# Feed-forward of a two-layer trunk: two instead of three blocks of gate and up by the plain product

## The chip, the core and the metric

The kernel runs on one core of one Trainium2 chip. The metric is the device time of one launch in microseconds (us), taken as the median of several runs; lower is better.

## What is computed

The reference is a trunk of two layers over 1024 latent tokens and 256 context tokens of width 1024. Each layer is a token mixer (a gating group, a windowed attention, a recurrent scan) followed by a feed-forward part. Only the feed-forward part matters here:

```python
def swiglu(h, w_gu, w_down):
    gu = h @ w_gu
    return (jax.nn.silu(gu[..., :D_FF]) * gu[..., D_FF:]) @ w_down
```

`h` has 1280 rows in the first layer (256 of context, 1024 latent) and 1024 in the second, `D_FF` is 2816, and everything is float32.

## The kernel before, in words

**Precision.** A float32 product is made of three products: each operand is split into a high part (a rounded copy, made by ScalarE) and a low part (the rest, by a subtraction on VectorE). `mm3` issues high times high, high times low and low times high. So one product of a 128x128 weight tile with 512 columns is three matmuls.

**Gate and up, in 22 blocks.** A block `f` is 128 columns of gate and the 128 columns of up that belong to them. Two ways of making it stand side by side:

- The *plain* way, `gu_group` (L1506): for each group of tokens (a group of 256 context tokens in the first layer alone, two of 512 latent tokens), 2 times 8 tiles of 128x128 with three matmuls each. For the latent tokens that is 2 x 2 x 8 x 3 = 96 matmuls of 512 columns.
- The way by *seven products of halves*, `visit` (L1604): the four products of a 2x2 block product are made by seven products (`operands` lists them), each with 4 tiles of 128x128 over 512 columns and three matmuls a tile: 7 x 4 x 3 = 84 matmuls of 512 columns. The context tokens go the plain way in both, with 48 matmuls of 256 columns.

**What the seven products need first.** `t_sums` (L1523) makes sums of parts of `h` on VectorE and splits them (tiles `tt`, by way of a temporary `tx`), for each of four slices `kk` of the width and for each of the two latent groups: eight pieces. `t_last` (L1549) then writes the last sum over a part of `h` that the plain way has read until then. `prep` (L1561) does the same for the weights of a block: it loads gate (`wq`) and up (`wu`), makes two sums of them on GpSimd (tiles `wq`), and splits the operands into `wh` and `wl` (ScalarE L1583, VectorE L1584), two of them ahead of the visit and two in it. Products 1 and 2 of a visit use the split of gate itself, and product 1 is the first of the visit.

**Space.** Large tiles lie in 33 numbered slots. `alloc` takes the slot that has been free the longest and `rel` puts it at the end of the queue; this is settled when the program is written, and a tile that takes over a slot waits on the chip until the last reader of the old one is done. When the sums come to the slice `kk = 3`, `h` has 16 slots, the output tile one, the weights' up half of block 1 two (tiles `wsh`, `wsl`, since the small ring `wh` of six is full), the `tt` tiles of the slices 0 to 2 nine, and the tiles `t4` two. The three `tt` tiles of slice 3 take the last three free slots, and the two `tx` tiles of that slice, one for each group, take the slots of `wsh` and `wsl`. Three slots for `prep` (`own`) are allocated after the sums: these are the same two slots, first that of the first group's `tx` (for the load of gate), then that of the second group's (for the first sum of weights), and then the slot of a `t4` tile (for the second sum, used by products 3 and 7).

**The order around the change** (L1770 to L1803). The plain blocks 0 and 1 go over the groups first, beside the norm of the next group and the sums. Then `after_two` runs: blocks 0 and 1 over the last group, the release of `wsh` and `wsl`, and then the further plain blocks (`range(2, NCL)`, so block 2 alone). Its steps are interleaved with the sums' steps by `weave`. Behind that stand `t_last`, `own`, the preparation of the first visited block, and the visits:

```python
        more = [(wget(0), wget(0)) for _ in range(2, NCL)]
        own = []
        nxt = prep(NCL, side, own)
...
        def after_two():
            yield from gu2(gb)
            for f in range(2):
                rel(*[z for w in wf[f] for z in w[2]])
            for f in range(2, NCL):
                yield from plain(f)
        weave(after_two(), both(sums(gb, (0, 1)), sums(ga, (2,)), sums(gb, (2,)), sums(ga, (3,)), sums(gb, (3,))))
        for kk in range(4):
            t_last(kk)
        own += [alloc("wq") for _ in range(3)]
        run(nxt)
```

The instructions of each engine run in one fixed order, which a scheduler settles when the program is built; loads and stores are issued in order on SyncE's queue. Results of a block go to memory (`actd`) and are read again by the product with `w_down`, which does not know how a block was made.

Of the kernel before, what the change touches and what calls it, by code (L numbers as in the profile page):

```python
# [34 lines left out]
NLATE = 5  # L35
FA = 6, 7, 8, 9
NP = 2
NCL = 3
DOWN = [(0, 21), (1, 2, 3), (4, 5, 6), (7, 8, 9), (10, 11, 12), (13, 14, 15), (16, 17), (18, 19, 20)]
PPW = 111  # L40
C_DECAY = 0.3032653298563167
# [52 lines left out]
def trunk(ctx: ExitStack, tc: tile.TileContext, x, ctxt, cc, w_mod, pp, w_in, w_out, lng, lnb, sgw, sink,  # L94
# [21 lines left out]
    def rel(*ss):  # L116
        for s in ss:
            free.append(s.i)
# [118 lines left out]
    def wget(ahead=2, slots=False):  # L237
        if not ready:
            emit_w(slots)
        r = ready.popleft()  # L240
        while len(ready) < ahead and plan and plan[0]:
            emit_w(slots)
        return r
# [17 lines left out]
    def mod_blocks(l, q, k):  # L261
        c = 2048 * q
        return [(w_mod[l, k * 128:(k + 1) * 128, c + z * 1024:c + (z + 1) * 1024], 0, 1024) for z in range(2)]

    def plan_gu(l, f):
        w = w_gu[l].rearrange("(k p) c -> p k c", p=128)
        plan.append((w[:, :, f * 128:(f + 1) * 128], 8, 128))
        plan.append((w[:, :, DFF + f * 128:DFF + (f + 1) * 128], 8, 128))
# [5 lines left out]
    for l in range(L):  # L274
# [9 lines left out]
        if l == 0:  # L284
            for k in range(8):
                plan.extend(mod_blocks(0, 2, k))
        for f in range(NCL):
            plan_gu(l, f)
# [248 lines left out]
    def layer(l):  # L537
# [1023 lines left out]
        def prep(f, side, own):  # L1561

            w = W()
            side.append(w)
            new = lambda i: sp.tile([128, NTOK], F32, tag=f"s{own[i].i}", name=nm("wq"))[:, :1024]
            g = new(0)
            u = wp.tile([128, 1024], F32, tag="wr", name=nm("wu"), bufs=2)
            wv = w_gu[l].rearrange("(k p) c -> p k c", p=128)
            for z, t in enumerate((g, u)):
                D.dma_start(t.rearrange("p (a b) -> p a b", a=8), wv[:, :, z * DFF + f * 128:z * DFF + (f + 1) * 128])  # L1570
            yield
            a, b = new(1), new(2)
            G.tensor_tensor(a[:, 0:512], u[:, 0:512], u[:, 512:1024], op=ALU.add)  # L1573
            G.tensor_tensor(a[:, 512:1024], a[:, 0:512], g[:, 0:512], op=ALU.subtract)
            yield
            G.tensor_tensor(b[:, 0:512], g[:, 0:512], u[:, 0:512], op=ALU.subtract)
            G.tensor_tensor(b[:, 512:1024], g[:, 512:1024], a[:, 512:1024], op=ALU.subtract)
            yield
            raw, w.hi, w.lo = (g, u, a, b), [None] * 4, [None] * 4

            def split(i):
                w.hi[i], w.lo[i] = (wp.tile([128, 1024], F32R, tag="wh", name=nm(x), bufs=6) for x in ("wh", "wl"))
                S.activation(w.hi[i], raw[i], AF.Copy)  # L1583
                V.tensor_tensor(w.lo[i], raw[i], f32(w.hi[i]), op=ALU.subtract)  # L1584
            split(0)
            yield
            split(2)
            yield
            w.late = [lambda: split(3), lambda: split(1)]
# [183 lines left out]
        side = []  # L1773
# [4 lines that stand above are left out]
        def plain(f):  # L1778
            w = more.pop(0)
            for gi in gord:  # L1780
                yield from gu_group(f, gi, w, ft)
            rel(*[z for x in w for z in x[2]])
# [7 lines that stand above are left out]
# [6 lines left out]
        wd = {}  # L1796
        for f in range(NCL, NFF):
            w = side.pop()
# [173 lines left out]
```

## Time and profile before

| | |
|---|---|
| median of 3 runs | 3268.1 us |
| lowest, highest | 3267.36, 3279.27 us |
| the profiled execution | 3278.91 us |
| its span | 3277.1 us |
| mean granted clock of TensorE | 0.979 |

The span is from the first to the last instruction of the profiled execution. In rows of a timeline, the first number is the start in us from the beginning of the span and the second the duration in us; "x2" stands for two instructions merged into one row. In square brackets stands how long the engine sat idle before it, and what released it. The ends of matmuls are modelled, and neighbours overlap: what one matmul costs in a stream is read from the distance of starts.

### The profile page before, as it was taken

The page shows a single profiled execution, that of the slowest core. Times are in us where ns is not written, and L with a number is a line of the kernel's source. Part 1 is how long each engine was busy: PE and PEld are TensorE (multiplying, and loading weights), DVE is VectorE, ACT ScalarE, POOL GpSimd, SP SyncE. Part 2 cuts the span into 40 slices and gives each one's busy share as a digit, 9 for nine tenths or more (in the row PEclk, how much of TensorE's full clock was granted, in tenths as well). Part 3 has the DMA queues.
Part 4 walks back from the last instruction along what each step waited for, and adds up shares of the span by engine and source line. Part 5 has one row for each costly group of instructions (what it writes and reads, how often), then busy time and mean ns, then how long its engine had stood idle before and what let it go on. Part 6 is the DMA issues. An engine that isn't in the chain of part 4 may idle for free. (4 is left out here: it accounts for less than half of the span.)

```text
span 3277.1 us, 51928 instructions
## 1 busy us (share of the span) xinstructions
PE 3163.4 (97%) x19892; PEld 2571.4 (78%) x19892; DVE 2022.1 (62%) x3966; ACT 1386.3 (42%) x2874; POOL 528.0 (16%) x598
## 2 busy tenths in 40 slices
PE   7998999999999999999999998999999999999998
PEld 4777988777788888886687777878777788888887
DVE  3457869676474555554455657779676666666556
ACT  4455477665342222222112555477665432333211
POOL 2103101132012222210001202001122122231000
PEclk9997999999999999999999989999999999999999
DMA  5784322445511222235722366412445222223232
GB/s 215 228 257 142 97 62 66 116 136 193 209 57 64 68 71 70 70 131 186 259 85 80 107 217 188 138 58 84 110 128 197 86 76 83 89 79 135 94 106 96
DMA packets 395175, 403.95 MB, mean 123 GB/s; under 512 B 113456, under 2 KB 334640, under 8 KB 394928
## 3 DMA queue, kind: packets, MB, share of 16 engines
q1 hardware_dynamic: 394928, 400.64, 37.7%
q8 instruction: 157, 2.57, 0.3%
q14 instruction: 90, 0.74, 0.1%
HBM read 279.97 MB, written 120.59 MB: 122 GB/s over the span
## 5 line engine op out<-in xcount | busy, mean ns | idle before, releaser
L147 PE MATMUL mm<-h,wh 128*128 128x512 f32 (+1 forms) x1424 | 423.9, 381 | 3.3 <-ACT ntmp L399 2.3
L147 PE MATMUL mm<-wh,h 128*128 128x256 f32 x1472 | 331.4, 301 | 0.8 <-DVE rtmp L954 0.8
L147 PE MATMUL dd<-h,wh 128*128 128x256 f32 (+1 forms) x1312 | 321.4, 336 | 1.3 <-DVE h L408 0.7
L147 PEld LDWEIGHTS mm<-h,wh 128*128 128x128 f32 x1424 | 260.1, 192 | 60.9 <-issue 10.8
L147 PE MATMUL mm<-h,wl 128*128 128x512 f32 (+1 forms) x712 | 268.6, 377 | 1.1 <-DVE wl L232 1.1
L147 PEld LDWEIGHTS mm<-wh,h 128*128 128x128 f32 x1472 | 255.6, 199 | 16.1 <-issue 15.2
L147 PEld LDWEIGHTS dd<-h,wh 128*128 128x128 f32 x1312 | 227.6, 191 | 29.4 <-DVE h L408 1.1
L1583 ACT ACTIVATE wh<-wq 128x1024 fp32r<-128x1024 f32 x114 | 121.0, 1061 | 302.3 <-PE dd L147 113.8
L147 PE MATMUL dd<-h,wl 128*128 128x256 f32 (+1 forms) x656 | 219.4, 334 | 0.0
L147 PE MATMUL mm<-wl,h 128*128 128x256 f32 x736 | 215.3, 292 | 1.8 <-DVE wl L232 1.8
L1584 DVE TENSOR_TENSOR wl<-wq,wh 128x1024 fp32r<-128x1024 f32 x114 | 141.3, 1240 | 114.3 <-ACT wh L1583 114.3
L147 PE MATMUL dd<-tt,wh 128*128 128x512 f32 x608 | 188.1, 391 | 0.0
L179 POOL TENSOR_TENSOR ss<-ss,mh_sb 128x1 f32<-128x1 f32 x74 | 50.6, 684 | 845.9 <-DVE ss L376 843.6
L147 PEld LDWEIGHTS mm<-h,wl 128*128 128x128 f32 x712 | 136.2, 191 | 26.3 <-issue 1.5
L1705 DVE TENSOR_TENSOR yac<-yac,mm 128x512 f32<-128x512 f32 x126 | 86.3, 685 | 112.1 <-PE mm L147 111.8
L147 PEld LDWEIGHTS mm<-wl,h 128*128 128x128 f32 x736 | 146.8, 199 | 6.4 <-issue 4.1
L1705 DVE TENSOR_TENSOR yac<-yac,xx 128x512 f32<-128x512 f32 x126 | 86.2, 684 | 92.8 <-PE xx L147 92.6
L1573 POOL TENSOR_TENSOR wq<-wu 128x512 f32<-128x512 f32 x38 | 49.2, 1295 | 561.7 <-DVE wl L1584 477.7
L147 PEld LDWEIGHTS dd<-h,wl 128*128 128x128 f32 x656 | 124.9, 190 | 12.4
L147 PEld LDWEIGHTS dd<-tt,wh 128*128 128x128 f32 x608 | 111.7, 188 | 21.3
L147 PE MATMUL u<-bC,bC 128*128 128x128 f32 (+1 forms) x640 | 119.6, 305 | 0.0
L147 PE MATMUL dd<-tt,wl 128*128 128x512 f32 x304 | 118.3, 389 | 0.0
(372 smaller groups left out, 7794.1 us busy)
## 6 DMA issues: line engine op xcount, KB each, us to landing
wm<-in_w_mod SPq DMA_DIRECT2D x80, 512.0 KB, 5.0
wr<-in_w_down SPq DMA_DIRECT2D x44, 512.0 KB, 4.3
wr<-in_w_in SPq DMA_DIRECT2D x38, 512.0 KB, 4.6
cb<-ao SPq DMA_DIRECT2D x76, 256.0 KB, 2.4
wu<-in_w_gu SPq DMA_DIRECT2D x38, 512.0 KB, 3.7
wq<-in_w_gu SPq DMA_DIRECT2D x38, 512.0 KB, 3.7
ao<-rk SPq DMA_DIRECT2D x58, 256.0 KB, 3.9
xs<-xr SPq DMA_DIRECT2D x28, 512.0 KB, 2.7
```

Of the source, the lines that this page charges most:

```text
L147: T.matmul(o, lhsT=lhsT, rhs=rhs, start=start, stop=stop, skip_group_check=parts)
L179: G.tensor_tensor(dst, src, mh[:, :n], op=ALU.pow)
L1573: G.tensor_tensor(a[:, 0:512], u[:, 0:512], u[:, 512:1024], op=ALU.add)
L1583: S.activation(w.hi[i], raw[i], AF.Copy)
L1584: V.tensor_tensor(w.lo[i], raw[i], f32(w.hi[i]), op=ALU.subtract)
L1705: V.tensor_tensor(yac[t].t[:, c], yac[t].t[:, c], ps, op=ALU.add)
```

## The change

One constant is lowered, so that the plain way makes blocks 0 and 1 and the seven products make blocks 2 to 21, in both layers.

```diff
-NCL = 3
+NCL = 2
```

It is used in four places: the plan of loads (`plan_gu`), the list `more`, the loop of `after_two`, and the first block of `prep` and of the loop of visits. The tile slots are handed out in the same order as before, since the plain block 2 allocates none.

## Rows read from the trace of the kernel before

**Rows 1.** The page: TensorE's share of the span, and its granted clock.
```profile
PE 3163.4 (97%) x19892; PEld 2571.4 (78%) x19892; DVE 2022.1 (62%) x3966; ACT 1386.3 (42%) x2874; POOL 528.0 (16%) x598
...
PEclk9997999999999999999999989999999999999999
```

**Rows 2.** Stretches A:B of the visits: length, then busy us (count) by engine, clock.
```profile
core 0: us, PE busy (x) PEld busy (x) DVE busy (x) ACT busy (x) POOL busy (x), PEclk, DMA share, GB/s
...
997.20:1469.50 472.30, 472.30 (x2509) 408.80 (x2508) 251.99 (x285) 119.79 (x154) 99.52 (x73) 1.00 0.24 77
...
2661.20:3022.90 361.70, 361.70 (x1597) 299.52 (x1596) 224.90 (x249) 112.89 (x136) 99.38 (x73) 1.00 0.28 90
```

**Rows 3.** Timeline of PE at the edges of plain block 2 and visits 3, 4.
```profile
969.42 0.39 PE L147 MATMUL dd<-h,wsl 128*128 128x512 f32 x1
969.65 0.40 PE L147 MATMUL dd<-h,wh 128*128 128x256 f32 x2
...
997.19 0.62 PE L147 MATMUL mm<-h,wh 128*128 128x512 f32 x2
...
1022.05 0.62 PE L147 MATMUL mm<-h,wh 128*128 128x512 f32 x2
...
2639.41 0.61 PE L147 MATMUL dd<-h,wh 128*128 128x512 f32 x2
...
2661.16 0.61 PE L147 MATMUL mm<-h,wh 128*128 128x512 f32 x2
...
2680.20 0.61 PE L147 MATMUL mm<-h,wh 128*128 128x512 f32 x2
```

**Rows 4.** Timeline of DVE: the sums of slice 3 and the first split of weights.
```profile
969.62 1.29 DVE L1531 TENSOR_TENSOR tx<-h,h 128x512 f32<-128x512 f32 x2 [7.24 <-PE dd L147]
...
974.91 0.68 DVE L1544 TENSOR_TENSOR tt<-tx,tt 128x512 fp32r<-128x512 f32 x1
...
978.14 0.69 DVE L1544 TENSOR_TENSOR tt<-tx,tt 128x512 fp32r<-128x512 f32 x1
980.37 2.33 DVE L1584 TENSOR_TENSOR wl<-wq,wh 128x1024 fp32r<-128x1024 f32 x1 [1.54 <-ACT wh L1583]
...
994.01 3.59 DVE L1554 TENSOR_TENSOR h<-t,h 128x512 fp32r<-128x512 f32 x4
...
2639.38 1.29 DVE L1531 TENSOR_TENSOR tx<-h,h 128x512 f32<-128x512 f32 x2 [7.00 <-PE dd L147]
...
2644.66 0.68 DVE L1544 TENSOR_TENSOR tt<-tx,tt 128x512 fp32r<-128x512 f32 x1
...
2650.10 1.78 DVE L1584 TENSOR_TENSOR wl<-wq,wh 128x1024 fp32r<-128x1024 f32 x1 [2.10 <-ACT wh L1583]
```

**Rows 5.** Timeline of SyncE's queue: the load of gate for the first visit.
```profile
975.65 0.38 SPq L1570 DMA_DIRECT2D wq<-in_w_gu  x1
...
2645.42 0.38 SPq L1570 DMA_DIRECT2D wq<-in_w_gu  x1
```

**Rows 6.** Timeline of ACT: the first split of gate, in both layers.
```profile
979.28 1.06 ACT L1583 ACTIVATE wh<-wq 128x1024 fp32r<-128x1024 f32 x1 [1.17 <-DMA wq<-in_w_gu]
...
2649.01 1.06 ACT L1583 ACTIVATE wh<-wq 128x1024 fp32r<-128x1024 f32 x1 [1.74 <-DMA wq<-in_w_gu]
```

**Rows 7.** Timeline of POOL: the first sum of weights.
```profile
978.96 1.30 POOL L1573 TENSOR_TENSOR wq<-wu 128x512 f32<-128x512 f32 x1 [42.34 <-DVE tt L1544]
980.34 1.29 POOL L1574 TENSOR_TENSOR wq<-wq,wq 128x512 f32<-128x512 f32 x1
```

**Rows 8.** Stretches around two other idle times of PE, columns as in group 2.
```profile
2028.90:2032.00 3.10, 0.00 (x0) 0.00 (x0) 2.60 (x6) 1.95 (x5) 2.69 (x4) 0.50 0.55 190
2032.00:2039.20 7.20, 7.17 (x28) 6.33 (x29) 7.10 (x15) 4.44 (x8) 2.04 (x4) 0.50 0.64 160
...
1476.00:1479.40 3.40, 3.37 (x8) 2.48 (x8) 3.40 (x4) 2.81 (x3) 0.00 (x0) 0.50 0.40 111
```

**Rows 9.** Timeline of PE: matmuls of 512 columns in the last of those stretches.
```profile
1477.48 0.63 PE L147 MATMUL xx<-wl,ah 128*128 128x512 f32 x1
1477.91 0.63 PE L147 MATMUL mm<-wh,ah 128*128 128x512 f32 x1
```

## The prediction

> **What bounds the kernel now.** I read the page first. TensorE (PE) is busy for 97% of the span and its clock is nearly always full [rows 1]: the sum of PE's work is the first thing to look at, and any hole in it the second. Then the stretches of the visits: PE is busy for all 472.30 us of them in the first layer and for all 361.70 us in the second, at clock 1.00, while VectorE (DVE) has 252 of 472 us and 225 of 362 [rows 2]. So a block made here costs what its matmuls cost. Last I read, engine by engine, the timeline between the two ways of making a block. There PE runs without a hole too [rows 3], but DVE, SyncE's queue, ScalarE (ACT) and GpSimd (POOL) do not work ahead of it: they begin at the moment at which plain block 1 ends, and finish while plain block 2 runs [rows 4 to 7]. The reader is to see that in before the third plain block is also the cover for that preparation.
>
> **What the change removes and adds on PE.** First layer: plain block 2 takes 997.19 - 969.65 = 27.54 us, a visit 1022.05 - 997.19 = 24.86 us [rows 3]. Second layer: 2661.16 - 2639.41 = 21.75 and 2680.20 - 2661.16 = 19.04 us [rows 3]. The visits keep that pace: 19 in 472.30 us are 24.86 each, and 19 in 361.70 are 19.04 [rows 2]. So the exchange gives 2.68 and 2.71 us, 5.4 us together. The count agrees: 12 matmuls of 512 columns fewer per layer, at 19.04 / 84 = 0.227 us apart.
>
> The Trainium skill, "TensorE: Matmul & The Clock Gate", section "Back-to-back issue gap", gives about 131 ns per matmul of 512 columns for a sustained stream of weight loads and matmuls. By that the exchange would be worth 24 x 0.131 = 3.1 us and the total 2.3 us higher. The trace disagrees with it, and the 0.227 us goes into the sum.
>
> Smaller edits, at nothing: two loads, two splits on ACT (1.06 us each) and two on DVE for block 2's plain weights go, and one preparation of a visit comes; these engines have room beside PE [rows 2]. The activations of the block run beside later matmuls in both ways. The later stages read the same blocks from memory.
>
> **The cover that goes.** The new first visit must wait for a chain, which starts with a slot. The first `tx` tile of slice 3 takes a slot of the weights of plain block 1, and DVE's row says so: the sum sat idle for 7.24 us and was released by PE at 969.62, where the last matmul on those weights (969.42) ends and block 2's first (969.65) begins [rows 3, 4]. The second layer repeats it: 7.00 us, released at 2639.38, against 2639.41 [rows 3, 4]. The queue of slots is the same after the change, so the wait stays, and it ends when the last plain matmul ends. From there, with times of before, first layer:
>
> - The first group's sums, 969.62 to 974.91 + 0.68 = 975.59 [rows 4]. DVE has its order, with the activation of block 1 and the second group's first sums between. Nothing of plain block 2 lies in this stretch, so it stays 5.97 us.
> - `own`'s first slot is this `tx` tile: the load of gate is issued at 975.65 [rows 5] and ACT, idle until the DMA, starts the split at 979.28 [rows 6]: 3.63 us.
> - ACT's split, 1.06 us [rows 6]. Now PE could start product 1: it has the high part, but its third matmul wants the low part.
> - DVE's low part, 980.37 + 2.33 = 982.70 [rows 4]. 2.33 instead of the 1.2 us that the others take, beside a POOL instruction [rows 7]; I keep the measured time, since POOL will do the same work there.
>
> Two matmuls fit into that last wait, 0.45 us. PE's hole is 982.70 - 0.45 - 969.65 = 12.6 us. Second layer: 2650.10 + 1.78 - 0.45 - 2639.41 = 12.0 us [rows 3, 4], with the same links at 2645.42 and 2649.01 [rows 5, 6]. If the low part took the usual 1.2 us, the holes would be 11.5 and 11.4.
>
> Is something else later still? `tt` of slice 3 is done at 978.14 + 0.69 = 978.83 [rows 4], before PE comes back. The first sum of weights on POOL waits for that `tx` (978.96) and takes two instructions of 1.3 us [rows 7]; two splits behind, at some 981.7 + 1.06 + 1.2 = 984, product 6 can start, and PE comes to it at 982.25 + 12 x 0.227 = 985.0 at the earliest, later in the first layer, where context matmuls lie between. The second sum of weights waits for `t_last`, which before ran at 994 [rows 4] because block 2 still read that part of `h`; without it, it fits into DVE's idle time ahead of 969.62. None is late, but the margin is about a microsecond.
>
> **The clock.** Behind a long hole PE comes back at half clock. The trace has one that ended at 2032.0: the granted clock was 0.50 (1.2 GHz of 2.4) in its last 3.1 us, with PE at 0.00, and for 7.2 us after it; another hole, which ended at 1476.0, left 3.4 us at 0.50 [rows 8]. In that one, matmuls of 512 columns start 1477.91 - 1477.48 = 0.43 us apart [rows 9] instead of 0.227, so a microsecond of such work loses 0.47 us. I count from the first matmul (980.4), take off the 2.3 or 1.8 us in which PE waits for the low part anyway, and have (3.4 - 2.3) x 0.47 = 0.5 to (7.2 - 1.8) x 0.47 = 2.5 us per layer. I take the middle, 1.5, as nothing tells which of the two it will be.
>
> **The sum.** First layer 12.6 + 1.5 - 2.68 = +11.4; second 12.0 + 1.5 - 2.71 = +10.8; together +22.2 us. The profiled execution took 3278.9 us, so its like would take 3301.1. The median of the runs is 10.8 us lower; the stretches here are at full clock and free of that difference, so I put the sum on the median: 3268.1 + 22.2 = 3290.3 us.
>
> **Rivals.**
> - *The chain is covered elsewhere* (faster or no change). The place is the idle 7 us of DVE ahead of 969.62 [rows 4]: if the sums of slice 3 had started some 12 us earlier, the load of gate would land before PE needs it, and only the 5.4 us would be seen: 3262.7. It decides whether that wait is the slot or only DVE's order. For it: the row names PE, not a tile. Against it: both layers release at the very edge of a block, the slots in the code say the same, and neither changes. 5%.
> - *A shorter hole* (no change that can be told). The low part takes 1.2 us, the load of gate lands a little sooner, and the clock is back after 3.4 us: 11.4 less 0.3, plus 1.0, less 2.7 per layer, is +9.4, so +19 in all; only if the hole also shrinks to about 10 us does the total fall to +16 or less: 3284 and below. For it: DMA has less beside it there. Against it: all links are rows of one chain. 17%.
> - *A longer chain.* The change lets `t_last` run earlier. If the order gives it to DVE ahead of the sums of slice 3 or of the low part, its four instructions (3.59 us [rows 4]) go into the chain, in both layers: +29, 3297. If the second product waits too, 1 to 2 us more each. 15%.
> - *It does not do what it says.* All four uses of the constant follow it, and the blocks meet only in memory; I see no place for this.
>
> **How the numbers follow.** The forecast has 63%, the rivals 5, 17 and 15%. A difference under 0.5%, about 16 us, can't be told from none here; the runs of before alone spread over 12 us. Slower by more than that: all of the forecast but the part lost to the spread, and all of the longer chain, 0.75. Within: the shorter hole and that part, 0.21. Faster by over 0.5% would need 16 us, which the exchange can't give: 0.04 covers surprises. The range: down to 3278, a shorter hole of some 8 us on a low run; up to 3305, the longer chain, or the forecast on a run as high as the highest of before (3279.3 + 22 = 3301). Left out are the first rival and the extremes, under 2 in 10.
>
> **What would show it.** In the changed kernel's timeline, PE's first `mm<-h,wh` of the visits should come some 12 us after the last `dd<-h,wsl`, once in each layer, released by ACT or DVE through the split of gate, with the clock at 0.50 behind it. The first sum of slice 3 on DVE should still be released by PE at that edge, the load of gate be issued some 6 us and split some 9.6 us after it. The visits should keep 24.86 and 19.04 us, 20 of them each. I would be wrong if the holes were under 8 us, or if the load of gate were issued before the last plain matmul.

## The result, and the profile after

| | before | changed |
|---|---|---|
| median | 3269.2 us (4 runs, 3267.36 to 3279.27) | 3299.93 us (4 runs, 3293.24 to 3303.86) |
| ratio | | 1.0085, 95% interval 1.0069 to 1.0101 |
| the profiled execution, its span | 3278.91, 3277.1 us | 3303.81, 3302.0 us |
| mean granted clock | 0.979 | 0.975 |

The changed kernel is slower, by 0.85%. Runs of one and the same kernel spread over up to 19 us here, so below the totals are given as ratios with their intervals, and single microseconds are read from the stage that the change touches.

The page first: as many microseconds of matmuls as before, in a longer span (PEld are TensorE's weight loads, which overlap its matmuls).

```profile
PE 3164.2 (96%) x19868; PEld 2570.2 (78%) x19868; DVE 2039.4 (62%) x3980; ACT 1391.8 (42%) x2880; POOL 541.8 (16%) x606
```

Against [rows 1], PE has 24 instructions less, the 12 matmuls per layer, and the same busy time, since a matmul at half clock (below) is busy for longer. The rest is in a hole. These are PE's timeline rows at the end of the plain blocks, at the first visit and at the second, in both layers:

```profile
971.21 0.39 PE L147 MATMUL dd<-h,wsl 128*128 128x512 f32 x1
982.41 1.22 PE L147 MATMUL mm<-h,wh 128*128 128x512 f32 x2 [10.81 <-ACT wh L1583]
984.41 0.80 PE L147 MATMUL mm<-h,wl 128*128 128x512 f32 x1 [0.78 <-DVE wl L1584]
...
1011.26 0.61 PE L147 MATMUL mm<-h,wh 128*128 128x512 f32 x2
...
2651.06 0.39 PE L147 MATMUL dd<-h,wsl 128*128 128x512 f32 x1
2662.04 1.22 PE L147 MATMUL mm<-h,wh 128*128 128x512 f32 x2 [10.59 <-ACT wh L1583]
2664.27 0.79 PE L147 MATMUL mm<-h,wl 128*128 128x512 f32 x1 [1.01 <-DVE wl L1584]
...
2685.13 0.62 PE L147 MATMUL mm<-h,wh 128*128 128x512 f32 x2
```

Where [rows 3] go from one block to the next without a gap, PE now stands still for 10.8 and 10.6 us, until ACT has split gate, and stops once more for the low part. The first visit then takes 1011.26 - 982.41 = 28.85 us and 2685.13 - 2662.04 = 23.09 us instead of 24.86 and 19.04. Counted from the end of the last plain matmul (0.23 us behind its start): 10.97 + 28.85 - 27.54 = +12.3 us in the first layer and 10.75 + 23.09 - 21.75 = +12.1 in the second, 24.4 together. The profiled executions are 24.9 apart.

The chain in the first layer, by the timelines of four engines. DVE:

```profile
967.54 2.05 DVE L1554 TENSOR_TENSOR h<-t,h 128x512 fp32r<-128x512 f32 x3 [4.74 <-ACT h L1553]
971.41 1.29 DVE L1531 TENSOR_TENSOR tx<-h,h 128x512 f32<-128x512 f32 x2 [1.81 <-PE dd L147]
...
976.70 0.69 DVE L1544 TENSOR_TENSOR tt<-tx,tt 128x512 fp32r<-128x512 f32 x1
...
982.39 1.97 DVE L1584 TENSOR_TENSOR wl<-wq,wh 128x1024 fp32r<-128x1024 f32 x1 [1.58 <-ACT wh L1583]
984.40 2.18 DVE L1584 TENSOR_TENSOR wl<-wq,wh 128x1024 fp32r<-128x1024 f32 x1
```

The load of gate on SyncE's queue, by its timeline:

```profile
977.45 0.38 SPq L1570 DMA_DIRECT2D wq<-in_w_gu  x1
```

The split of gate, in ACT's timeline:

```profile
981.30 1.06 ACT L1583 ACTIVATE wh<-wq 128x1024 fp32r<-128x1024 f32 x1 [1.22 <-DMA wq<-in_w_gu]
```

The end of the first sum of weights and the start of the second, in POOL's timeline:

```profile
982.01 1.27 POOL L1574 TENSOR_TENSOR wq<-wq,wq 128x512 f32<-128x512 f32 x1
983.23 2.26 POOL L1576 TENSOR_TENSOR wq<-wq,wu 128x512 f32<-128x512 f32 x1
```

It is the chain of [rows 4 to 6], link by link: the sum is released by PE at 971.41, 0.2 us behind the start of the last plain matmul, gate is loaded 6.0 us later, and split 3.85 us after that. Three pieces of `t_last` found room ahead of it, at 967.54. The low parts of gate and of the first sum take 1.97 and 2.18 us on DVE beside POOL's sums, and a part of these takes 2.26 us. Nothing new stands in the chain; only the cover is gone.

The clock, in stretches of the same two places: the hole, the first part of the first visit, and the rest of it (length, then busy us by engine, and the granted clock behind them):

```profile
core 0: us, PE busy (x) PEld busy (x) DVE busy (x) ACT busy (x) POOL busy (x), PEclk, DMA share, GB/s
971.40:982.40 11.00, 0.20 (x1) 0.00 (x0) 9.22 (x20) 4.38 (x7) 2.17 (x2) 0.70 0.22 72
982.40:989.50 7.10, 6.30 (x16) 4.62 (x17) 4.80 (x3) 2.53 (x3) 6.59 (x4) 0.50 0.05 11
989.50:1011.20 21.70, 21.70 (x118) 18.86 (x118) 9.71 (x11) 4.45 (x6) 6.69 (x5) 1.00 0.24 70
...
2662.00:2668.90 6.90, 5.85 (x13) 4.17 (x14) 4.58 (x3) 2.11 (x2) 6.82 (x4) 0.51 0.03 8
```

PE comes back at half clock (1.2 GHz) and stays there for 7 us in each layer, as in the longer of [rows 8]. The later visits are dense at clock 1.00 as in [rows 2].

### The profile page after: what moved, and what is told of

Its sections match the earlier page's. It is cut to its first block, busy times and chain, and to the rows that moved or that the text cites. A ratio compares the mean times of both kernels' runs of the same rounds, so it can differ in the third digit from the quotient of the medians.

```text
span 3302.0 us, 51904 instructions
## 1 busy us (share of the span) xinstructions
PE 3164.2 (96%) x19868; PEld 2570.2 (78%) x19868; DVE 2039.4 (62%) x3980; ACT 1391.8 (42%) x2880; POOL 541.8 (16%) x606
## 5 line engine op out<-in xcount | busy, mean ns | idle before, releaser
L147 PE MATMUL mm<-h,wh 128*128 128x512 f32 (+1 forms) x1456 | 442.2, 388 | 24.3 <-ACT wh L1583 21.4
L147 PEld LDWEIGHTS mm<-h,wh 128*128 128x128 f32 x1456 | 271.2, 195 | 84.7 <-ACT wh L1583 22.3
L147 PE MATMUL dd<-h,wh 128*128 128x256 f32 (+1 forms) x1200 | 287.6, 331 | 1.9 <-DVE h L408 1.3
L147 PE MATMUL mm<-h,wl 128*128 128x512 f32 (+1 forms) x728 | 279.0, 383 | 2.9 <-DVE wl L1584 1.8
L147 PEld LDWEIGHTS dd<-h,wh 128*128 128x128 f32 x1200 | 207.4, 191 | 26.2 <-DVE h L408 1.9
L1584 DVE TENSOR_TENSOR wl<-wq,wh 128x1024 fp32r<-128x1024 f32 x120 | 150.6, 1255 | 111.3 <-ACT wh L1583 111.3
L147 PE MATMUL dd<-tt,wh 128*128 128x512 f32 x640 | 198.1, 391 | 0.0
L147 PE MATMUL dd<-h,wl 128*128 128x512 f32 (+1 forms) x600 | 197.8, 330 | 0.0
L147 PEld LDWEIGHTS dd<-h,wl 128*128 128x128 f32 x600 | 114.7, 191 | 10.2
```

The lines of the kernel that those rows point to most:

```text
L147: T.matmul(o, lhsT=lhsT, rhs=rhs, start=start, stop=stop, skip_group_check=parts)
```

## The experiments

Theory: from the end of the plain blocks, PE waits for a chain that begins with a slot, the one of block 1's weights. Rivals: PE waits for the plain work's end as such or for an order of instructions; the long first visit comes from late operands and not from the clock; and a part of the difference is only the spread of runs. The table holds the stage, from the last transposition ahead of the blocks' last group (PE's last row of L397) to the start of block 4's visit, both layers added, read from PE's timeline of each profile.

| kernel | stage, us | against before | time, ratio to before |
|---|---|---|---|
| before | 158.5 | | |
| changed | 182.9 | +24.4 | 1.0085 (1.0069 to 1.0101) |
| changed again | 181.4 | +22.9 | 1.0074 (1.0058 to 1.0089) |
| hole filled | 178.4 | +19.9 | 1.0055 (1.004 to 1.007) |
| gate in another slot | 172.7 | +14.2 | 1.0046 (1.0034 to 1.0058) |
| gate of block 1 in slots | 176.0 | +17.5 | 1.0047 (1.0031 to 1.0063) |
| block 1 first | 164.1 | +5.6 | 1.0016 (1.000 to 1.0031) |
| both of these edits | 158.1 | -0.4 | 1.001 (1.000 to 1.002) |
| both, additions on GpSimd | 160.8 | +2.3 | 1.0013 (1.0001 to 1.0024) |
| both, subtraction on GpSimd | 161.3 | +2.8 | 1.0014 (1.000 to 1.0028) |
| three plain blocks, both edits | 158.5 | 0.0 | 1.000 (0.9989 to 1.0011) |
| four plain blocks | 163.9 | +5.4 | 1.0022 (1.0012 to 1.0033) |

**The changed kernel again.**

> The changed kernel once more, beside the others on one chip. Theory: hole and long first visit repeat (10.6 to 11.0 us of idle time and 28.8 and 23.1 us), and it is 20 to 30 us over before, 1.006 to 1.009. Rival (part of the difference was the spread of runs): the stage between the plain blocks and the second visit keeps its 24.4 us more, and the total is under 1.006.

The hole came back (10.7 and 10.4 us), and the first visits took 29.2 and 21.5 us. The difference is not the spread of runs. These are the rows behind the short first visit of the second layer, from the timelines of PE, DVE and POOL and from the stretches:

```profile
2658.36 1.22 PE L147 MATMUL mm<-h,wh 128*128 128x512 f32 x2 [10.44 <-ACT wh L1583]
2659.61 0.80 PE L147 MATMUL mm<-h,wl 128*128 128x512 f32 x1
```

```profile
2658.34 1.23 DVE L1584 TENSOR_TENSOR wl<-wq,wh 128x1024 fp32r<-128x1024 f32 x1 [1.21 <-ACT wh L1583]
```

```profile
2658.33 2.36 POOL L1574 TENSOR_TENSOR wq<-wq,wq 128x512 f32<-128x512 f32 x1
```

```profile
2658.30:2663.00 4.70, 4.61 (x10) 3.22 (x11) 2.41 (x2) 1.06 (x2) 4.67 (x3) 0.51 0.02 5
```

Here the low part took 1.23 us and POOL's sum the longer time, so PE came to the low part 1.25 us behind its first matmul, not 2.23 as in the first run (2664.27 - 2662.04). That is 1.0 of the 1.6 us by which this visit is shorter. The other 0.6 us are the clock, which was at half speed for some 4.7 us instead of 6.9.

**The hole filled.**

```diff
+        fill = d_t()
+        for n in range(46):
+            mm(fill[:, 0:512], h2[0][n % 4].t[:, 0:128], h2[0][4 + n % 4].t[:, 0:512], n == 0, n == 45)
         own += [alloc("wq") for _ in range(3)]
```

> Two plain blocks, and 46 matmuls of 512 columns that nobody reads between the last plain block and the first visit, in each layer: some 10.4 us of work in a hole of 10.8. Theory (after the hole PE works at half clock, and this is what lengthens the first visit by 4 us): with the hole filled the clock stays at 1.00, the first visit takes 26.4 us in the first layer (24.86 and the wait for the low part, some 1.5) and 20.9 in the second instead of 28.84 and 23.08; the kernel comes out some 5 us under the changed one, about 20 over before. Rival (the first visit is long because its operands come late): it stays at 28.8 and 23.1, and the time is that of the changed kernel, some 25 to 28 over before.

PE's timeline at the end of the filling and at the second visit, and the stretches of filling and first visit:

```profile
977.17 0.73 PE L147 MATMUL mm<-h,wh 128*128 128x512 f32 x2 [0.48 <-ACT wh L1583]
...
1003.47 0.61 PE L147 MATMUL mm<-h,wh 128*128 128x512 f32 x2
```

```profile
966.10:977.10 11.00, 10.60 (x47) 8.45 (x45) 9.20 (x19) 4.38 (x7) 2.19 (x2) 1.00 0.23 72
977.20:1003.40 26.20, 25.19 (x132) 21.63 (x133) 15.24 (x13) 6.88 (x8) 13.27 (x9) 1.00 0.21 61
```

The chain takes as long as without the filling, but the clock stays at 1.00 and the first visits fall to 26.30 and 20.83 us, as the theory had it. So of the long first visits, 28.85 - 26.30 = 2.55 and 23.09 - 20.83 = 2.26 us are put down to the clock, and 1.44 and 1.79 us to the wait for late operands. This is a difference of two runs, and PE's order is not quite the same in them: with the filling, a matmul of a later product stands ahead of gate's low part and waits for the first sum of weights. The changed kernel's own rows give nearly the same shares: PE came to the low part 984.41 - 982.41 = 2.00 and 2.23 us behind its first matmul, 1.55 and 1.78 us more than two matmuls at full clock take, which leaves 2.4 and 2.3 us for the clock. Dead work in the hole makes the stage 3.0 to 4.5 us shorter than in the two runs of the changed kernel; the totals lean the same way, but their intervals overlap.

**Gate in another slot.**

```diff
-        new = lambda i: sp.tile([128, NTOK], F32, tag=f"s{own[i].i}", name=nm("wq"))[:, :1024]
+        new = lambda i: sp.tile([128, NTOK], F32, tag=f"s{own[(i + 2) % 3].i}", name=nm("wq"))[:, :1024]
```

> Two plain blocks; the three slots of the weights' preparation change roles: gate is loaded into the slot of a t4 tile, which is free when the second piece of t_last is done, and the two sums of weights take the two slots that the tx tiles of slice 3 leave. Theory (a chain of slot, load and split): the load of gate is issued near the last plain matmul, some 2 us ahead of it, PE begins product 1 some 2 to 3 us after the last plain matmul and stops a second time, ahead of product 6, for the first sum of weights: 3 us in the first layer, 5 in the second. Holes and the long first visit together cost some 7 and 8.5 us instead of 15 each; about 11 us over before. Rival (PE's first matmul waits for the sums of slice 3 themselves, not for gate): the hole stays near 10.8 us, and the time is that of the changed kernel.

PE's timeline at the first visit:

```profile
973.78 0.73 PE L147 MATMUL mm<-h,wh 128*128 128x512 f32 x2 [2.19 <-ACT wh L1583]
...
978.91 0.80 PE L147 MATMUL mm<-h,wl 128*128 128x512 f32 x1 [4.16 <-DVE wl L1584]
```

The first matmul comes 2.3 us after the plain blocks, with slice 3's sums unfinished: it waits for gate alone, and the rival falls. The second stop is for another reason than the one expected: the low part of gate stands behind the first group's sums in DVE's order (it starts at 977.63). 14.2 us are left instead of 11, and the clock fell in the second stop (0.50 behind it).

**The last reader of the weights half a block, and a whole block, earlier.**

```diff
-        wf = [(wget(0), wget(0)), (wget(0), wget(0, True))]
+        wf = [(wget(0), wget(0)), (wget(0, True), wget(0))]
```

> Two plain blocks; the weights that lie in slots are gate of block 1 instead of up of block 1, so that their last reader comes half a block (5.4 us) earlier. Theory (slot): the first sum of slice 3 starts 5.4 us ahead of the last plain matmul, the hole is 5.4 us shorter, about 5.5, and the time some 12 us over before. Rival (end of the plain work as such): the sum starts at the last plain matmul and nothing changes, 25 to 28 us over before.

```diff
-            for f in range(2):
+            for f in (1, 0) if gi == gord[-1] else (0, 1):
                 yield from gu_group(f, gi, wf[f], ft)
```

> Two plain blocks; over the last group of tokens block 1 is made ahead of block 0, so that the weights that lie in slots have their last reader one block (10.9 us) earlier. No work is added or left out. Theory (the first sum of slice 3 waits for the slot of these weights): that sum starts some 10.9 us ahead of the last plain matmul, the hole shrinks from 10.8 us to some 2, the clock stays at 1.00, the first visits take about 25 and 19.5 us, and the kernel comes to 3265 to 3269, within a few us of before. Rival (the sum waits for the end of the plain work as such, or stands behind it in the order): the sum still starts at the last plain matmul and the time stays some 25 to 28 us over before.

With gate of block 1 in slots, first layer, DVE's timeline at the first sum of slice 3:

```profile
965.92 1.29 DVE L1531 TENSOR_TENSOR tx<-h,h 128x512 f32<-128x512 f32 x2 [3.17 <-PE dd L147]
```

PE's timeline from the last plain matmul on, in the same run:

```profile
971.16 0.39 PE L147 MATMUL dd<-h,wl 128*128 128x512 f32 x1
975.77 1.22 PE L147 MATMUL mm<-h,wh 128*128 128x512 f32 x2 [4.23 <-ACT wh L1583]
...
981.32 0.80 PE L147 MATMUL xx<-tt,wh 128*128 128x512 f32 x1 [3.89 <-ACT wh L1583]
```

And POOL's timeline, the first sum of weights:

```profile
974.91 3.93 POOL L1573 TENSOR_TENSOR wq<-wu 128x512 f32<-128x512 f32 x1 [36.55 <-DVE tt L1544]
```

With block 1 first, DVE's timeline at the same sum and at the first split of weights:

```profile
959.11 1.29 DVE L1531 TENSOR_TENSOR tx<-h,h 128x512 f32<-128x512 f32 x2 [0.40 <-PE dd L147]
...
968.13 4.07 DVE L1554 TENSOR_TENSOR h<-t,h 128x512 fp32r<-128x512 f32 x3
972.13 4.51 DVE L1584 TENSOR_TENSOR wl<-wq,wh 128x1024 fp32r<-128x1024 f32 x2
```

And PE's timeline at its first visit, which begins where the plain blocks end:

```profile
970.02 0.67 PE L147 MATMUL mm<-h,wh 128*128 128x512 f32 x2
...
972.80 0.49 PE L147 MATMUL xx<-tt,wh 128*128 128x512 f32 x1 [1.88 <-ACT wh L1583]
974.48 0.79 PE L147 MATMUL mm<-h,wl 128*128 128x512 f32 x1 [1.19 <-DVE wl L1584]
```

The sum starts 971.16 + 0.23 - 965.92 = 5.5 us ahead of the plain blocks' end in the one run and 970.02 - 959.11 = 10.9 us ahead in the other. Moving the last reader of the slot moves the chain by as much, so the wait is the slot's. The rival falls.

DVE's timeline in the first of these runs, beside POOL's sum:

```profile
974.68 1.90 DVE L1554 TENSOR_TENSOR h<-t,h 128x512 fp32r<-128x512 f32 x3
976.49 1.23 DVE L1584 TENSOR_TENSOR wl<-wq,wh 128x1024 fp32r<-128x1024 f32 x1
```

The stage came out above the theory's in both, by 5 us in the first run and by 5 to 8 in the second, and the rows tell why. In the first run the first sum of weights took 3.93 us on POOL beside a full DVE, and PE's order has a matmul of a later product (`xx<-tt`) ahead of gate's low part, so PE waited for that sum as well; the clock fell. In the second, `t_last` stands ahead of the low part on DVE (968.13, 4.07 us for three pieces that take 2.05 alone), which is the mechanism of the prediction's longer chain, and more than five microseconds a layer stay (first visits of 30.09 and 24.82 us). In its second layer it is the first run's wait again, 3.84 us until the first sum of weights is split. The clock did not stay at 1.00 either: it was 0.76 and 0.56 on average in the 3.2 us behind these waits.

**Both edits together.**

> Two plain blocks, with block 1 made ahead of block 0 over the last group and gate of block 1, not its up, in slots: the last reader of these weights comes 16.3 us ahead of the last plain matmul. No work is added or left out. Theory (slot, and t_last ahead of the first low part in DVE's order as the rest of the hole in the run with the order alone): the sums of slice 3 start some 16 us ahead of the last plain matmul, gate is split before t_last can run, PE goes from the last plain matmul to the first visit with less than 1 us of idle time, the first visits take 24.9 to 25.5 and 19.0 to 19.7 us, and the kernel is faster than before by up to the 5.4 us of the exchange (ratio 0.998 to 1.000). Rival (another wait, the second sum of weights or the ring of split tiles, takes the place of the slot): 3 to 5 us of idle time stay in each layer and the kernel is at 1.001 to 1.002 of before.

The stretches ahead of the first visit, in the two layers:

```profile
937.00:969.00 32.00, 31.96 (x142) 26.13 (x140) 31.91 (x66) 12.39 (x23) 3.46 (x3) 1.00 0.12 42
2599.00:2632.00 33.00, 32.37 (x143) 26.47 (x141) 32.90 (x67) 13.47 (x24) 3.82 (x3) 1.00 0.12 41
```

DVE's timeline, first layer, at the first sum of slice 3, at `t_last` and at the splits of weights:

```profile
955.10 0.69 DVE L1531 TENSOR_TENSOR tx<-h,h 128x512 f32<-128x512 f32 x1
...
965.24 2.39 DVE L1554 TENSOR_TENSOR h<-t,h 128x512 fp32r<-128x512 f32 x2
967.55 2.32 DVE L1584 TENSOR_TENSOR wl<-wq,wh 128x1024 fp32r<-128x1024 f32 x1
969.79 3.47 DVE L1554 TENSOR_TENSOR h<-t,h 128x512 fp32r<-128x512 f32 x2
```

PE's timeline, the stops in the first visits of the two layers:

```profile
969.93 0.50 PE L147 MATMUL mm<-h,wl 128*128 128x512 f32 x1 [0.96 <-DVE wl L1584]
...
2632.57 0.50 PE L147 MATMUL mm<-h,wl 128*128 128x512 f32 x1 [1.20 <-DVE wl L1584]
...
2637.10 0.50 PE L147 MATMUL dd<-tt,wl 128*128 128x512 f32 x1 [1.50 <-DVE wl L1584]
```

PE goes over into the first visit without a gap and at full clock, and the first visits take 26.47 and 22.38 us. The stage is the shortest of all runs with two plain blocks, but the first visits are not the 24.9 to 25.5 and 19.0 to 19.7 us expected: PE stops for low parts, which come from DVE, and DVE has worked for 31.91 of the 32.00 us ahead of the visit, and 32.90 of 33.00. The slot is out of the way: the first sum of slice 3 starts 968.35 - 955.10 = 13.3 us ahead of the visit, not 16.3, with no idle time of DVE before it. And `t_last` was not outrun. Two of its pieces run ahead of gate's low part and two more ahead of the next one, which in the second layer is what PE waits for the second time. How much of the 1.6 and 3.3 us is the late sums and how much is `t_last` is not separated. They and the exchange's 5.4 us cancel, and the ratio of 1.001 shows no gain over before.

**Some of the sums on GpSimd.** In the run with both edits (the first pair of lines shortened at the dots):

```diff
-                V.tensor_tensor(X.t[:, 512 * i:512 * i + 512].rearrange(...)
+                (G if i and kk < 3 else V).tensor_tensor(X.t[:, 512 * i:512 * i + 512].rearrange(...)
```

> The run with two plain blocks, block 1 first over the last group and its gate in slots, and in it the second of the two 512-column additions of a piece of sums on GpSimd instead of VectorE, for the slices 0 to 2 (six pieces a layer, 0.6 us of VectorE each, 1.3 us on GpSimd alone). Theory (VectorE, busy for 31.9 of the 32 us ahead of the first visit, is now what the low part waits for): up to 3.6 us less on VectorE, the first visits fall from 26.47 and 22.38 to 25 and 19.5 us, and the kernel comes to 3 to 5 us under before (ratio 0.9985 to 0.999). Rival (the two engines slow each other when both work, as the split beside GpSimd's sums took 2.3 instead of 1.2 us): VectorE's instructions beside GpSimd's grow by about as much as was taken from it, the first visits stay or grow, ratio 1.000 to 1.003.

```diff
-            V.tensor_tensor(t4, b21, t2, op=ALU.subtract)
+            G.tensor_tensor(t4, b21, t2, op=ALU.subtract)
```

> The same run with two plain blocks and both edits, and in it the last subtraction of each piece of sums (128x256, 0.34 us of VectorE, eight a layer) on GpSimd, whose result only t_last needs. Theory (VectorE is the bound): 2 to 2.7 us less on VectorE, the first visits near 25.5 and 20.5 us, ratio 0.999 to 1.000. Rival (the engines slow each other, or GpSimd's sums of weights now wait behind it): first visits of 26.5 and 22.4 us or more, ratio 1.001 or more.

Neither helped. One of the additions on GpSimd, from POOL's timeline of the first of these runs:

```profile
947.65 4.22 POOL L1531 TENSOR_TENSOR tx<-h,h 128x512 f32<-128x512 f32 x1 [3.24 <-DVE tt L1544]
```

It took 4.22 us where the weights' sums of the same size take 1.29 alone [rows 7]; in the other run a subtraction on GpSimd took up to 7.27 us. The first visits are 27.4 and 23.1 us, and in the other run 28.6 and 22.1. The other run also took DVE down to 27.75 of the 32.00 us and 28.02 of the 33.00 ahead of the visits without a gain, so a full DVE is not all that was left. That work moved from DVE to POOL in this stage buys nothing is shown; how much of it is the two engines waiting for each other (last section) and how much the new order of the queues is not separated.

**Three plain blocks with both edits, and four plain blocks.**

> Three plain blocks as before, with both edits of the run beside it (order over the last group, gate of block 1 in slots). It has the cover in any case. Theory: neither edit does anything where plain block 2 covers the chain; the time is that of before (0.999 to 1.001), and some 5 us over the run beside it, which is the exchange of one block by itself. Rival (the edits help or harm by themselves): it differs from before by more than 3 us, in the stage of the plain blocks.

> Four plain blocks instead of three, nothing else. Theory (a plain block costs 2.7 us more than a visit in each layer, and the cover is complete with three already): visits and plain blocks keep 24.86 and 27.54 us (19.04 and 21.75), no idle time of PE between them, and the time is about 5.4 us over before (1.0016). Rival (three blocks do not cover all of it yet): it is less than 2 us over before, or faster.

With the cover of a third plain block the edits change nothing (stage 158.51 against 158.50), and a fourth plain block costs 5.4 us in the stage. So the exchange is worth what [rows 3] say, and three blocks cover the chain entirely. The 131 ns per matmul that the prediction quotes from the Trainium skill ("TensorE: Matmul & The Clock Gate", section "Back-to-back issue gap") would make it 3.1 us; the measured 5.4 us go with the 0.227 us of the trace.

## Why the prediction was right

Direction and mechanism held; the time was given as 3290.3 us and measured as 3299.93, within the range but nearer to its upper end. Step by step:

- **The exchange**, 5.4 us: 5.4 in the run with four plain blocks.
- **The slot as the head of the chain**: shown by the two runs that moved the last reader. That gate is the next link is shown by the run that gave it another slot.
- **The hole up to the low part**, 12.6 and 12.0 us. Measured the same way, the low part's first matmul comes 984.41 - 971.44 and 2664.27 - 2651.29 us behind the plain blocks, 13.0 in both, and 12.5 less the two matmuls. The run with the filled hole agrees: 10.97 + 1.44 = 12.4 and 10.75 + 1.79 = 12.5. The slower split beside POOL's sums, which the prediction kept, is part of it: 1.97 us in the first layer, where 2.33 was put, and 2.19 in the second, where 1.78 was put and the hole came out half a microsecond short.
- **The clock**, 1.5 us a layer, is the term that was mis-sized: 2.55 and 2.26 by the filled hole, 2.4 and 2.3 by the changed kernel's own rows. The row with the longer stretch at 0.50 was the one that applied, and the middle between the two rows was too low. The second run of the changed kernel, with 1.7 us by the same count in its second layer, shows that it varies.
- **The sum**: the terms measured in the profiles are 24.9 of holes and late operands, 4.8 of clock, less 5.4, so 24.3, against 22.2. The measured ratio, 1.0069 to 1.0101, is 23 to 33 us. The medians of the table are 30.7 us apart, 6.3 more than the stage holds; the two profiled executions differ by 0.5 us outside the stage, so this is put down to the spread of four runs against four, which is not shown. The median of before on which the sum was put rests on few runs: 19, 27 and 23 later ones have medians of 3275.73, 3273.11 and 3272.85 us, within 3262.43 to 3280.96, and the forecast's 22.2 us on top of those come closer to what was measured. The changed kernel run again beside the 27 had 3298.02 us, 24.9 over them.
- **The rivals**: the cover elsewhere and the shorter hole did not come. The longer chain did not either, as `t_last` found DVE's idle time as forecast; it appeared where an edit moved the chain over it. One slip in the chances: the first rival's 3262.7 us lie within 0.5% of before, so its 5% belonged to "within", where the stated 0.21 leaves room for one point of it.

## What to carry to other kernels

Ask of a block of work that looks dear what else runs while it does: here the dear way of making one block covered a chain of sums, a load and a split that could start only when a buffer came free. Follow that chain back to its first release, and look for the last reader of that buffer; moving the reader took away nearly the whole loss here (the stage from +24.4 to -0.4 us), but it won nothing over the cover, since the engine behind it was then full. And count a long hole of PE twice, once as idle time (10.6 to 10.8 us here) and once as the matmuls at half clock behind it (some 2.4 us here).

## What the runs showed of the hardware

VectorE and GpSimd took turns where both had additions or subtractions of two tiles in SBUF: the one that came second waited, and the first kept its own time. In the kernel before, POOL's sum at 980.34 took its usual 1.29 us, and DVE's split, begun 0.03 us after it, 2.33 instead of 1.23 [rows 4, 7]. In the second run of the changed kernel the two began within 0.01 us, DVE came first with 1.23 us, and POOL's sum took 2.36. With gate of block 1 in slots, POOL's sum began in the middle of a stretch of DVE without a pause, whose rows kept 1.90 us for three and 1.23; it ended 1.1 us behind that stretch and took 3.93. In the twelve profiles, 43 splits on DVE began while a sum of weights that had not itself been held up was under way on POOL, and every one of them ended 1.08 to 1.12 us behind that sum. So 2.26, 3.93 and 4.22 us on GpSimd instead of 1.29 are mostly waiting, and work moved from DVE to POOL does not run beside DVE's work of this kind. The prediction had one side of this, the split of 2.33 us; it took it as a fixed cost of the link, and which engine comes first can change from one execution to the next.
